# A two-layer mixer block: modulation sums on VectorE, neighbourhood q and k projected in transposed form, and recurrent gates whose sigmoid follows in SBUF

## The chip, the cores and the metric

The kernel runs on one core of one Trainium2 chip. The metric is the device time of one execution in microseconds (us), as the median of several runs; the profile is of one execution of its own.

## The reference

Two layers work on 1024 latent tokens and 256 context tokens (1280 rows in all) of 1024 channels. Each layer is one modulated block:

```python
shift, scale, gate = split(silu(cond) @ w_mod + b_mod, 3)    # for c and for c_ctx: two streams
p = (layer_norm(x) * (1 + scale) + shift) @ w_in             # 7072 columns
ya = neighbourhood_attention(q, k, v)                        # A: 4 heads of 64, scale 1/8
yb = mla(...);  yc = rglru(...);  yd = gqa(...)              # B, C, D
out = sum(sigmoid(m[i]) * ((y[i] * silu(z[i])) @ w_branch[i]) for i in range(4)) @ w_out
x = layer_norm(alpha * x + gate * out) * ln_g + ln_b
```

Branch C is a gated linear recurrence in both directions: `r = sigmoid(x @ w_a + b_a)`, `i = sigmoid(x @ w_x + b_x)`, `a = exp(-8 r softplus(-lambda))`, `u = sqrt(1 - a*a) * i * x`, and a scan `h = a h + u`. The second layer needs no context output, so its merge has 1024 rows where the first has 1280.

## The kernel before

Everything is float32. Most matrix products are made of three TensorE products of rounded parts (`mm_a`, L297 to L301, with the x tile standing and the weights moving; `mm_b`, L303 to L309, with the weights standing and x moving): a high part made by a ScalarE copy (`hi`) and a low part, the difference, made by VectorE (`lo`). Weights come from HBM in pieces of 128x512 (SP's queue, L278), are split in the same way (L263 on ScalarE, L264 on VectorE), and have two raw buffers and six pairs of split ones in the later half of a layer.

A layer runs through these stages, with the names that the trace shows: `g_proj`; then `m_proj`, `a_proj` (both projections of the branches) woven with `lru` (branch C); then the attentions `g_att`, `m_att`, `a_att`; then `merge` (gates, branch products and their sum), `last` and `outp`. `weave` runs two generators in turn by the given weights, which only sets the order of recording; a scheduler then reorders within what dependencies allow, and each engine works through its own list in order.

*Modulation.* The first modulation is made at the start. The other three (gate of layer 0, shift and scale of layer 1, gate of layer 1; 4096 columns in all) are made by `later_mods`, woven into the merge of layer 0. For each of 64 pieces of `w_mod` (tile `wm`, three buffers of the tag `q`), the two condition columns `sc` stand in TensorE and the weights move through (L188). At the end ScalarE copies the two rows out of PSUM (L194), 32 small transposes turn them into columns (L197), and VectorE adds the bias (L199). The second layer's merge has none of this.

*Neighbourhood projection.* `a_steps` projects q and k of branch A for each tile of 128 rows with x standing, copies them out of PSUM on ScalarE (L808, L809), turns each 128x128 block by a TensorE transpose (`put_t`, L348), splits it and writes both parts to HBM, since the attention wants channels on the partitions.

*Recurrent branch.* For each of two channel halves and two directions, two gates are made. Each has three products of 256, 512 and 512 columns in PSUM, and the sigmoid with its bias takes each out (L515). Then follow Tanh (L522), Exp (L523) and Sqrt (L528) on 128x1280. ScalarE loads a function table (ACT_TABLE_LOAD) where the next function isn't in the loaded one.

*Merge.* For each of four branches and eight output chunks `c`: with a gate chunk not made ahead, 24 products of x with gate weights per group of rows (`merge__mm`), then 6 of the branch (`wide`, three banks of PSUM used in turn). ScalarE makes the sigmoid (L999). VectorE multiplies (L1003 in the first branch, L1005 later), and VectorE or GpSimd adds to the sum `acc` (L1006: GpSimd for the chunks whose gate was made ahead).

Of the kernel before, what the change touches and what calls it, by code (L numbers as in the profile page):

```python
# [8 lines left out]
F32 = mybir.dt.float32  # L9
F32R = mybir.dt.float32r  # L10
AF = mybir.ActivationFunctionType
ALU = mybir.AluOpType
# [24 lines left out]
W_A = 30  # L37
# [10 lines left out]
def hybrid_kernel(ctx: ExitStack, tc, a):  # L48
# [124 lines left out]
    def modulation(l, base, ncols, out, stage, sw):  # L173
# [18 lines left out]
        for j in range(g):  # L192
            row = tmp()
            act.copy(row[0:2, :w_], acc[32 * j:32 * j + 2, :w_])  # L194
            for i in range(w_ // 128):
# [5 lines left out]
                          bm[:, :n, None].to_broadcast([128, n, 2]), ALU.add)  # L201
        if n == 16:
            dve.tensor_scalar(mc[:, :, 8:16], mc[:, :, 8:16], 1.0, None, ALU.add)
# [111 lines left out]
    def layer(l, xh, xl, need_ctx, gate, finish, side, ahead=None):  # L315
# [157 lines left out]
        def lru_steps():  # L473
            cw, cb, ba, bx, ca, cn = lru["cols"][l]
            for c in range(2):
# [30 lines left out]
                for d in range(2):  # L506
                    ri = []
                    for gi, bias in enumerate((ba, bx)):
                        wh, wl = gh[:, 2 * d + gi, :], gl[:, 2 * d + gi, :]
                        o = slot(s="lrug")  # L510
                        for g in groups:
                            gs = slice(g[0], g[0] + g[1])
                            ps = sbank()
                            mm_b(ps[:, :g[1]], [(wh, wl)], lambda k: (xch[:, gs], xcl[:, gs]))
                            act.activation(o[:, gs], ps[:, :g[1]], AF.Sigmoid, bias=bias[:, 2 * d + c:2 * d + c + 1])  # L515
                        ri.append(o)
                        yield
                    r, i = ri
# [282 lines left out]
        def a_steps():  # L801
            wa = load_rows(w_in, C_A, 512)
            prev = None
            for t, ps in project(wa, lambda t: 0 if t >= q0t else 256, 512):
                c0 = 0 if t >= q0t else 256
                y = tmp()
                if c0 == 0:
                    act.activation(y[:, :256], ps[:, :256], AF.Copy, scale=0.125)  # L808
                act.copy(y[:, 256:], ps[:, 256:])  # L809
                if prev:  # L810
                    put_t(*prev)
                prev = qk_a, t, c0 // 128, [y[:, c:c + 128] for c in range(c0, 512, 128)]
                yield
            put_t(*prev)
# [196 lines left out]
        weave((f"merge{l}", merge(), 4 * KC * len(qgroups)), (f"mod{l}", side, 68))  # L1011
# [150 lines left out]
    def raw_w():  # L1162
        return tp.tile([128, 512], F32, tag="q", name=nm("wm"), bufs=3)

    def later_mods():
        yield from modulation(0, 2048, 1024, gate0, raw_w, 512)
        yield from modulation(1, 0, 2048, mc1, raw_w, 512)
        yield from modulation(1, 2048, 1024, gate1, raw_w, 512)
# [102 lines left out]
```

## Time and profile before

| | |
|---|---|
| median of 3 runs | 2924.19 us (2923.29 to 2927.37) |
| profiled execution | 2926.0 us, of which the span is 2924.2 us |
| mean granted TensorE clock | 0.979 |
| TensorE busy | 2782.2 us (95%) |
| VectorE, ScalarE, GpSimd busy | 1503.1, 1219.3, 420.1 us |
| merge of layer 0 | 1082.3 to 1486.3 us of the span |
| merge of layer 1 | 2540.0 to 2823.4 us of the span |

The span runs from the first to the last instruction of the profiled execution. An engine's busy time is the sum over its instructions, and of a fraction of the span; what an engine off the path does costs nothing by itself, so a stage's own rows have to be read.

### The profile page before, as it was taken

Reading aid. Unit: us, or ns where it says so; the run is one execution under the profiler, and the core shown is the slowest. Engines: PE = TensorE matmul, PEld = TensorE weight load, DVE = VectorE, ACT = ScalarE, POOL = GpSimd, SP = SyncE. Lnnn points to the kernel's source line nnn. Section 1 sums busy time; section 2 is a strip of 40 time slices with the busy share of each in tenths; the row PEclk is TensorE's granted clock in tenths of the full one; section 3 lists DMA queues with packets and bytes.
Section 4 is the critical chain, followed back from the end, with each engine's and each line's share of the span. In section 5 each row is a group of like instructions: output and inputs, shape, how many; then the busy total and the mean of one; then the engine's idle time right before and its main releaser. Section 6 shows DMA issues by size and latency. Waiting matters only on the chain. (4 is left out here: it accounts for less than half of the span.)

```text
span 2924.2 us, 40179 instructions
## 1 busy us (share of the span) xinstructions
PE 2782.2 (95%) x14458; PEld 2248.4 (77%) x14458; DVE 1503.1 (51%) x3085; ACT 1219.3 (42%) x2617; POOL 420.1 (14%) x507
## 2 busy tenths in 40 slices
PE   7978999999999999999999797999999999999998
PEld 4766788888888887777767586788888888777776
DVE  5645435555455652233358655445555556533357
ACT  4353535445455552222224435535545455522230
POOL 1211011110111100111222121011111111001131
PEclk9988999999999999999999898999999999999999
DMA  7424232222223324333332333342222333222232
GB/s 249 119 66 146 79 103 84 85 85 85 92 86 124 103 94 128 100 121 120 122 89 87 99 102 102 105 122 87 85 88 78 113 115 110 93 87 88 89 113 88
DMA packets 240424, 301.83 MB, mean 103 GB/s; under 512 B 27488, under 2 KB 160096, under 8 KB 240224
## 3 DMA queue, kind: packets, MB, share of 16 engines
q1 hardware_dynamic: 134368, 225.58, 24.5%
q10 hardware_dynamic: 105856, 73.68, 8.1%
q8 instruction: 114, 1.87, 0.3%
q14 instruction: 86, 0.70, 0.1%
HBM read 217.11 MB, written 82.07 MB: 102 GB/s over the span
## 5 line engine op out<-in xcount | busy, mean ns | idle before, releaser
L307 PE MATMUL merge__mm<-xh,merge__whi 128*128 128x512 f32 (+1 forms) x640 | 242.2, 378 | 0.9 <-ACT a_att__tmp L934 0.9
L308 PE MATMUL merge__mm<-xl,merge__whi 128*128 128x512 f32 (+1 forms) x640 | 238.6, 373 | 0.0
L309 PE MATMUL merge__mm<-xh,merge__wlo 128*128 128x512 f32 (+1 forms) x640 | 238.5, 373 | 0.0
L313 DVE TENSOR_TENSOR m_att__pl<-m_att__t,m_att__ph 128x384 fp32r<-128x384 f32 (+1 forms) x248 | 122.0, 508 | 117.5 <-ACT m_att__ph L312 78.8
L1005 DVE TENSOR_TENSOR merge__tmp<-wide,merge__tmp 128x512 f32<-128x512 f32 (+1 forms) x120 | 76.5, 637 | 194.8 <-PE wide L309 173.7
L263 ACT CAST merge__whi<-merge__wraw 128x256 fp32r<-128x256 f32 (+1 forms) x128 | 65.8, 514 | 249.3 <-PE merge__mm L308 172.9
L1006 POOL TENSOR_TENSOR merge__acc<-merge__acc,merge__tmp 128x512 f32<-128x512 f32 (+1 forms) x60 | 79.0, 1317 | 574.8 <-DVE merge__tmp L1005 574.7
L313 DVE TENSOR_TENSOR g_att__pl<-g_att__t,g_att__ph 128x384 fp32r<-128x384 f32 (+1 forms) x228 | 112.8, 515 | 88.3 <-ACT g_att__ph L312 56.0
L312 ACT CAST m_att__ph<-m_att__t 128x384 fp32r<-128x384 f32 (+1 forms) x248 | 105.2, 440 | 115.0 <-PE m_att__t L584 105.3
L307 PEld LDWEIGHTS merge__mm<-xh,merge__whi 128*128 128x128 f32 x640 | 120.2, 188 | 42.8 <-issue 16.5
L264 DVE TENSOR_TENSOR merge__wlo<-merge__wraw,merge__whi 128x256 fp32r<-128x256 f32 (+1 forms) x128 | 72.0, 563 | 131.8 <-ACT merge__whi L263 124.8
L309 PEld LDWEIGHTS merge__mm<-xh,merge__wlo 128*128 128x128 f32 x640 | 120.3, 188 | 23.8 <-issue 0.4
L308 PEld LDWEIGHTS merge__mm<-xl,merge__whi 128*128 128x128 f32 x640 | 120.3, 188 | 22.4
L307 PE MATMUL wide<-merge__uh,merge__whi 128*128 128x256 f32 (+1 forms) x320 | 127.9, 400 | 9.3 <-DVE merge__tmp L1005 6.7
L312 ACT CAST g_att__ph<-g_att__t 128x384 fp32r<-128x384 f32 (+1 forms) x228 | 98.2, 446 | 83.3 <-PE g_att__t L584 78.7
L307 PE MATMUL a_att__mm<-xh,a_att__whi 128*128 128x512 f32 (+1 forms) x320 | 123.7, 387 | 0.0
L641 DVE TENSOR_SCALAR_CACHE_REDUCE g_att__p<-wide 128x1280 f32<-128x1280 f32 (+1 forms) x72 | 98.6, 1369 | 45.9 <-PE wide L639 35.7
L641 DVE TENSOR_SCALAR_CACHE_REDUCE m_att__p<-wide 128x1280 f32<-128x1280 f32 (+1 forms) x72 | 98.7, 1371 | 42.3 <-PE wide L639 41.8
L309 PE MATMUL a_att__mm<-xh,a_att__wlo 128*128 128x512 f32 (+1 forms) x320 | 120.0, 377 | 0.0
L308 PE MATMUL a_att__mm<-xl,a_att__whi 128*128 128x512 f32 (+1 forms) x320 | 120.0, 375 | 0.0
L308 PE MATMUL wide<-merge__ul,merge__whi 128*128 128x256 f32 (+1 forms) x320 | 119.7, 374 | 0.0
L299 PE MATMUL a_proj__mm<-a_proj__whi,xh 128*128 128x256 f32 (+1 forms) x320 | 110.3, 346 | 9.9 <-ACT a_proj__whi L263 9.8
(418 smaller groups left out, 7908.4 us busy)
## 6 DMA issues: line engine op xcount, KB each, us to landing
merge__wraw<-in_w_chunks_dram SPq DMA_DIRECT2D x64, 256.0 KB, 2.9
mod__wm<-in_w_mod_dram SPq DMA_DIRECT2D x64, 256.0 KB, 3.1
g_proj__wm<-in_w_mod_dram SPq DMA_DIRECT2D x16, 512.0 KB, 9.6
a_att__wraw<-in_w_chunks_dram SPq DMA_DIRECT2D x32, 256.0 KB, 2.8
merge__wraw<-in_w_branch_dram SPq DMA_DIRECT2D x64, 128.0 KB, 2.0
merge__tmp<-start__gates SPq DMA_DIRECT2D x32, 256.0 KB, 3.2
merge__tmp<-outp__gates SPq DMA_DIRECT2D x32, 256.0 KB, 3.4
g_att__wraw<-in_w_chunks_dram SPq DMA_DIRECT2D x28, 256.0 KB, 2.7
```

Source lines behind the costliest of these rows:

```text
L263: act.copy(hi[:, :n], raw[:, :n])
L264: (pool if by_pool else dve).tensor_sub(lo[:, :n], raw[:, :n], hi[:, :n])
L299: pe.matmul(ps, xh, wh[:, n0:n1], start=first and k == 0, stop=False)
L307: pe.matmul(ps, wh, xh, start=first and k == 0, stop=False)
L308: pe.matmul(ps, wh, xl, start=False, stop=False)
L309: pe.matmul(ps, wl, xh, start=False, stop=last and k == nk - 1)
L312: act.copy(hi, src)
L313: dve.tensor_sub(lo, src, hi)
L641: dve.tensor_scalar(pt[:, :nk], wide[:, :nk], -scale, None, ALU.mult, ALU.min, accum_out=nb)
L1005: dve.tensor_mul(sgm[:, :g[1]], pb[:, :g[1]], sgm[:, :g[1]])
L1006: (pool if w is None else dve).tensor_add(acc[c][:, gs], acc[c][:, gs], sgm[:, :g[1]])
```

## The change

- `later_mods` calls a new `modulation_apart`. The condition values become per-partition factors on VectorE: per block of 512 columns and per stream, one TENSOR_SCALAR and seven SCALAR_TENSOR_TENSOR of 128x512 add the eight pieces of `w_mod` up (L223 and L225 of the changed kernel; sums in the tags `ph` and `pl`, three and two buffers). Four TensorE products per block and stream with the sum standing and one column of `mhalf` (each -0.5) moving add over the partitions (L230). One VectorE instruction applies -2 and the bias (L233). The steps' weight in the weave goes from 68 to 76, and W_A from 30 to 32.
- `a_steps` makes q and k with the weights standing (`mm_b`), so that channels come out on the partitions; ScalarE takes the high part out of PSUM, VectorE the low part, and two DMAs write them. The transposes and the copies ahead of them are gone for this branch.
- `lru` takes the gates out of PSUM with Identity and the bias (L548), and two sigmoids of 128x1280 in SBUF follow (L553).

```diff
-W_A = 30
+W_A = 32
...
+    def modulation_apart(l, base, ncols, out):
+        acc = ps_v.tile([128, 512], F32, tag="pv", name=nm("pm"))
+        n = ncols // 128
+        bm = lc.tile([128, 16], F32, tag="bm", name=nm("bm"))
+        sp.dma_start(bm[:, :n], a["b_mod"][l, :, base // 128:base // 128 + n])
+        for h in range(ncols // 512):
+            sums = [tp.tile([128, 512], F32, tag=tag, name=nm("ms"), bufs=b) for tag, b in (("ph", 3), ("pl", 2))]
+            for k in range(KC):
+                w = raw_w()
+                sp.dma_start(w, a["w_mod"][l, k * 128:(k + 1) * 128, base + h * 512:base + (h + 1) * 512])
+                for s in range(2):
+                    if k == 0:
+                        dve.tensor_scalar(sums[s], w, sc[:, k, s:s + 1], None, ALU.mult)
+                    else:
+                        dve.scalar_tensor_tensor(sums[s], w, sc[:, k, s:s + 1], sums[s], ALU.mult, ALU.add)
+                yield
+            for s in range(2):
+                for c in range(4):
+                    o = s * n + 4 * h + c
+                    pe.matmul(acc[:, o:o + 1], sums[s][:, c * 128:(c + 1) * 128], mhalf[:, 0:1], start=True, stop=True)
+            yield
+        mc = lc.tile([128, 2, 16], F32, tag="modc", name=nm("modc"), bufs=4)
+        dve.scalar_tensor_tensor(mc[:, :, :n], acc[:, :2 * n].rearrange("p (s n) -> p s n", s=2), -2.0,
+                                 bm[:, None, :n].to_broadcast([128, 2, n]), ALU.mult, ALU.add)
...
-                            act.activation(o[:, gs], ps[:, :g[1]], AF.Sigmoid, bias=bias[:, 2 * d + c:2 * d + c + 1])
+                            act.activation(o[:, gs], ps[:, :g[1]], AF.Identity, bias=bias[:, 2 * d + c:2 * d + c + 1])
                         ri.append(o)
                         yield
+                    for o in ri:
+                        act.activation(o, o, AF.Sigmoid)
...
         def a_steps():
             wa = load_rows(w_in, C_A, 512)
-            prev = None
-            for t, ps in project(wa, lambda t: 0 if t >= q0t else 256, 512):
-                c0 = 0 if t >= q0t else 256
-                y = tmp()
-                if c0 == 0:
-                    act.activation(y[:, :256], ps[:, :256], AF.Copy, scale=0.125)
-                act.copy(y[:, 256:], ps[:, 256:])
-                if prev:
-                    put_t(*prev)
-                prev = qk_a, t, c0 // 128, [y[:, c:c + 128] for c in range(c0, 512, 128)]
+            items = [(c, g) for c in range(4) for g in (qgroups if c < 2 else groups)]
+            def part(c, g, ps, ks):
+                xs = xs_g(g)
+                ws = [(wh[:, c * 128:(c + 1) * 128], wl[:, c * 128:(c + 1) * 128]) for wh, wl in wa]
+                mm_b(ps[:, :g[1]], [ws[k] for k in ks], lambda j: xs(ks[j]), ks[0] == 0, ks[-1] == KC - 1)
+            def keep(c, g, ps):
+                n, scale = g[1], 0.125 if c < 2 else 1.0
+                hi = tp.tile([128, 512], F32R, tag="ph", name=nm("th"), bufs=3)
+                lo = tp.tile([128, 512], F32R, tag="pl", name=nm("tl"), bufs=2)
+                act.activation(hi[:, :n], ps[:, :n], AF.Copy, scale=scale)
+                dve.scalar_tensor_tensor(lo[:, :n], ps[:, :n], scale, hi[:, :n], ALU.mult, ALU.subtract)
+                for d, s in enumerate((hi, lo)):
+                    act.dma_start(qk_a[d, c, :, g[0]:g[0] + n], s.bitcast(F32)[:, :n])
+            for c, g in items[:-2]:
+                ps = mm()
+                part(c, g, ps, list(range(KC)))
+                keep(c, g, ps)
                 yield
-            put_t(*prev)
...
-        weave((f"merge{l}", merge(), 4 * KC * len(qgroups)), (f"mod{l}", side, 68))
+        weave((f"merge{l}", merge(), 4 * KC * len(qgroups)), (f"mod{l}", side, 76))
...
     def later_mods():
-        yield from modulation(0, 2048, 1024, gate0, raw_w, 512)
-        yield from modulation(1, 0, 2048, mc1, raw_w, 512)
-        yield from modulation(1, 2048, 1024, gate1, raw_w, 512)
+        yield from modulation_apart(0, 2048, 1024, gate0)
+        yield from modulation_apart(1, 0, 2048, mc1)
+        yield from modulation_apart(1, 2048, 1024, gate1)
```

The scheduler's order changes with it. Below, a row is a line of the program, an operation, the tile written and the tiles read, with the columns of the output, in the order in which the engine takes them.

TensorE, before, some 20 us into the merge of layer 0 (between the first and the third chunk; `wide` is a branch product, L188 a modulation piece):

```order
L309 MATMUL wide<-merge__uh_10946,merge__wlo_10975 128x512
L188 MATMUL mod__pm_11013<-mod__wm_11109,sc 2x256 x2
L188 MATMUL mod__pm_11013<-mod__wm_11123,sc 2x256 x2
L188 MATMUL mod__pm_11013<-mod__wm_11137,sc 2x256
L307 MATMUL wide<-merge__uh_10932,merge__whi_11094 128x256
```

Three pieces of modulation stand between two branch products; such stops recur through the whole merge.

TensorE in the changed kernel, some 53 rows into the same merge (L340 to L342 are L307 to L309 of before):

```order
L341 MATMUL merge__mm_11013<-xl,merge__whi_10958 128x512
L342 MATMUL merge__mm_11013<-xh,merge__wlo_10959 128x512
L230 MATMUL mod__pm_11003<-mhalf,mod__ms_11006 128x1 x4
L230 MATMUL mod__pm_11003<-mhalf,mod__ms_11007 128x1 x4
L340 MATMUL merge__mm_11051<-xh,merge__whi_10952 128x512
```

No row of L188 is left in this merge; the rows of L230 are 16 in all, two for each of the eight blocks, and stand in seven places.

VectorE, before, in the merge's first branch (L1003 takes a `wide` bank out of PSUM, L264 makes the low part of weights):

```order
L1003 TENSOR_TENSOR merge__acc_10978<-wide,merge__tmp_11058 128x512
L264 TENSOR_TENSOR merge__wlo_11318<-merge__wraw_11315,merge__whi_11317 128x512
L1003 TENSOR_TENSOR merge__acc_11098<-wide,merge__tmp_11099 128x256
L1003 TENSOR_TENSOR merge__acc_11098<-wide,merge__tmp_11113 128x512
L1003 TENSOR_TENSOR merge__acc_11098<-wide,merge__tmp_11127 128x512
```

Nothing but the low parts of weights stands between the multiplications that free the banks.

VectorE in the changed kernel at the same place (L1056 is L1003 of before, L297 is L264):

```order
L1056 TENSOR_TENSOR merge__acc_10968<-wide,merge__tmp_11050 128x512
L297 TENSOR_TENSOR merge__wlo_11320<-merge__wraw_11317,merge__whi_11319 128x512
L225 SCALAR_TENSOR_TENSOR mod__ms_11756<-mod__wm_11796,sc,mod__ms_11756 128x512
L1056 TENSOR_TENSOR merge__acc_11094<-wide,merge__tmp_11095 128x256
L225 SCALAR_TENSOR_TENSOR mod__ms_11755<-mod__wm_11835,sc,mod__ms_11755 128x512
L225 SCALAR_TENSOR_TENSOR mod__ms_11756<-mod__wm_11835,sc,mod__ms_11756 128x512
L1056 TENSOR_TENSOR merge__acc_11094<-wide,merge__tmp_11109 128x512
L225 SCALAR_TENSOR_TENSOR mod__ms_11755<-mod__wm_11856,sc,mod__ms_11755 128x512
L225 SCALAR_TENSOR_TENSOR mod__ms_11756<-mod__wm_11856,sc,mod__ms_11756 128x512
L225 SCALAR_TENSOR_TENSOR mod__ms_11755<-mod__wm_11882,sc,mod__ms_11755 128x512
L1056 TENSOR_TENSOR merge__acc_11094<-wide,merge__tmp_11119 128x512
```

Each PSUM bank that VectorE frees now has modulation sums ahead of it. They begin some 45 rows ahead of the first L1056, among the last instructions of `a_att`: from there to the second group of the merge's third chunk, 49 of the 128 sums stand in VectorE's list, and 25 of the 64 pieces of `w_mod` belong to them.

ScalarE, before, in one direction of the recurrent branch:

```order
L515 ACTIVATE lru__lrug_1628<-wide,lrucols 128x512
L523 ACT_TABLE_LOAD
L523 ACTIVATE lru__lrug_1524<-lru__lrug_1524,lrusp_311 128x1280
L515 ACT_TABLE_LOAD
L515 ACTIVATE lru__lrug_1628<-wide,lrucols 128x512
```

The last eviction of the second gate stands behind the Exp and a table load of its own.

ScalarE in the changed kernel at the same place (L548 is L515 of before, L559 is L523; L756 and L789 belong to `m_proj`):

```order
L548 ACTIVATE lru__lrug_1628<-wide,lrucols 128x512
L559 ACT_TABLE_LOAD
L559 ACTIVATE lru__lrug_1615<-lru__lrug_1615,lrusp_311 128x1280
L548 ACTIVATE lru__lrug_1628<-wide,lrucols 128x512
L756 ACTIVATE m_proj__tmp_1887,m_proj__ss_377_1888<-m_proj__mm_1862 128x128
L553 ACT_TABLE_LOAD
L553 ACTIVATE lru__lrug_1628<-lru__lrug_1628 128x1280
L789 COPY m_proj__mbuf_1690<-wide 128x256
```

The eviction after the Exp no longer has a table load ahead of it; the load stands ahead of the sigmoid, and both stand ahead of a copy of `m_proj`. Both programs have 39 table loads on ScalarE.

## Rows read from the trace of the kernel before

**Rows 1.** The page, busy time of TensorE, share of the span, instructions.

```profile
...
PE 2782.2 (95%) x14458; PEld 2248.4 (77%) x14458; DVE 1503.1 (51%) x3085; ACT 1219.3 (42%) x2617; POOL 420.1 (14%) x507
```

**Rows 2.** Busy time by stretch: stretch, length, engines, granted clock, DMA share, GB/s.

```profile
...
117.00:265.00 148.00, 125.67 (x611) 105.66 (x609) 78.26 (x178) 68.02 (x165) 28.05 (x45) 0.91 0.34 96
...
1082.30:1486.30 404.00, 398.49 (x1972) 297.40 (x1970) 144.81 (x249) 113.01 (x239) 57.99 (x53) 0.99 0.39 120
...
2540.00:2823.40 283.40, 278.07 (x1161) 216.22 (x1162) 117.68 (x188) 91.08 (x176) 44.94 (x35) 0.99 0.31 97
```

**Rows 3.** The same view of the first merge, tiles mod__pm, then mod__t alone.

```profile
...
1082.30:1486.30 404.00, 39.62 (x192) 5.41 (x192) 5.20 (x12) 0.99 0.39 120
...
1082.30:1486.30 404.00, 3.88 (x32) 2.94 (x32) 0.58 (x3) 0.99 0.39 120
```

**Rows 4.** Timeline of TensorE in the first merge: start, duration, engine, line, operation.

```profile
...
1118.87 0.39 PE L309 MATMUL wide<-merge__uh,merge__wlo 128*128 128x512 f32 x1
1119.19 0.60 PE L188 MATMUL mod__pm<-mod__wm,sc 128*2 128x256 f32 x4
1119.72 0.50 PE L307 MATMUL merge__mm<-xh,merge__whi 128*128 128x512 f32 x1
1120.06 0.40 PE L308 MATMUL merge__mm<-xl,merge__whi 128*128 128x512 f32 x1
```

**Rows 5.** Waits of TensorE in the first merge: us, times, longest.

```profile
...
PE wide L307 <- DVE merge__tmp L1005: 3.2, 5, 0.8
```

**Rows 6.** Instructions of L1077: count, duration min/median/max in ns.

```profile
...
L1077 DVE SCALAR_TENSOR_TENSOR outp__Y<-outp__Y,outp__mv,outp__ln_g x36: 735/748/756, 1528.0 to 2918.6; 128x512 f32<-128x512 f32 x36
```

**Rows 7.** Busy time by stretch, around the start of the first merge.

```profile
...
1062.00:1119.00 57.00, 56.23 (x302) 44.70 (x300) 18.90 (x36) 15.94 (x32) 1.23 (x2) 1.00 0.38 125
```

**Rows 8.** Loads of the tile mod__wm.

```profile
...
DMA to landing us min/median/max: 2.5/3.1/9.1
```

**Rows 9.** Instructions of L1006 in the first merge, durations in ns.

```profile
...
L1006 DVE TENSOR_TENSOR merge__acc<-merge__acc,merge__tmp x36: 424/685/1225, 1186.9 to 1476.0; 128x512 f32<-128x512 f32 x24, 128x256 f32<-128x256 f32 x12
L1006 POOL TENSOR_TENSOR merge__acc<-merge__acc,merge__tmp x34: 727/1296/1806, 1203.5 to 1478.0; 128x512 f32<-128x512 f32 x22, 128x256 f32<-128x256 f32 x12
```

**Rows 10.** Waits of SP's queue in the first merge.

```profile
...
SPq L278 <- DVE merge__wlo L264: 136.8, 39, 10.3
SPq L185 <- PE mod__pm L188: 106.6, 34, 8.1
```

**Rows 11.** Busy time of the tile a_proj__t in both layers.

```profile
...
sum 558.00, PE 13.06 PEld 9.45 DVE 13.13 ACT 11.57; mean PE 6.53 PEld 4.73 DVE 6.56 ACT 5.78
```

**Rows 12.** Timeline of TensorE around one set of those transposes.

```profile
...
294.28 0.60 PE L348 MATMUL a_proj__t<-ident,a_proj__tmp 128*128 128x128 f32 x4
294.63 0.48 PE L307 MATMUL wide<-xh,lru__whi 128*128 128x512 f32 x1
294.96 0.40 PE L308 MATMUL wide<-xl,lru__whi 128*128 128x512 f32 x1
```

**Rows 13.** Waits of TensorE, projections of the first layer.

```profile
...
PE a_proj__mm L299 <- ACT a_proj__whi L263: 9.8, 4, 6.2
PE wide L299 <- ACT lru__lrug L515: 6.7, 2, 3.7
...
PE wide L307 <- ACT lru__lrug L515: 1.7, 1, 1.7
```

**Rows 14.** Waits of TensorE, projections of the second layer.

```profile
...
PE wide L299 <- ACT lru__lrug L515: 3.0, 1, 3.0
PE wide L307 <- ACT lru__lrug L515: 2.6, 2, 1.7
```

**Rows 15.** Timeline of ScalarE, one direction of the recurrent branch.

```profile
...
185.30 1.28 ACT L515 ACT_TABLE_LOAD   x1
186.59 0.69 ACT L515 ACTIVATE lru__lrug<-wide,lrucols 128x512 f32<-128x512 f32 x1
...
189.29 1.27 ACT L528 ACTIVATE lru__lrut<-lru__lrut 128x1280 f32<-128x1280 f32 x1
```

More of the change, by code (lines that the diff above doesn't have):

```diff
@@ L201, in modulation, with raw_w @@
                           bm[:, :n, None].to_broadcast([128, n, 2]), ALU.add)
+        if n == 16:
+            dve.tensor_scalar(mc[:, :, 8:16], mc[:, :, 8:16], 1.0, None, ALU.add)
+        out["m"] = mc
+        yield
+    def raw_w():
+        return tp.tile([128, 512], F32, tag="q", name=nm("wm"), bufs=3)
+    def modulation_apart(l, base, ncols, out):
[18 more added lines that the diff above has]
+                    pe.matmul(acc[:, o:o + 1], sums[s][:, c * 128:(c + 1) * 128], mhalf[:, 0:1], start=True, stop=True)
+            yield
+        mc = lc.tile([128, 2, 16], F32, tag="modc", name=nm("modc"), bufs=4)
+        dve.scalar_tensor_tensor(mc[:, :, :n], acc[:, :2 * n].rearrange("p (s n) -> p s n", s=2), -2.0,
+                                 bm[:, None, :n].to_broadcast([128, 2, n]), ALU.mult, ALU.add)
         if n == 16:
@@ L802, in a_steps @@
             wa = load_rows(w_in, C_A, 512)
-            prev = None
-            for t, ps in project(wa, lambda t: 0 if t >= q0t else 256, 512):
-                c0 = 0 if t >= q0t else 256
-                y = tmp()
-                if c0 == 0:
-                    act.activation(y[:, :256], ps[:, :256], AF.Copy, scale=0.125)
-                act.copy(y[:, 256:], ps[:, 256:])
-                if prev:
-                    put_t(*prev)
-                prev = qk_a, t, c0 // 128, [y[:, c:c + 128] for c in range(c0, 512, 128)]
-                yield
-            put_t(*prev)
+            items = [(c, g) for c in range(4) for g in (qgroups if c < 2 else groups)]
[15 more added lines that the diff above has]
+                keep(c, g, ps)
+                yield
+            last = [(c, g, mm()) for c, g in items[-2:]]
+            for k in range(KC):
+                for c, g, ps in last:
+                    part(c, g, ps, [k])
+            for c, g, ps in last:
+                keep(c, g, ps)
+                yield
             wv = load_rows(w_in, C_AV, 256)
@@ L1160, in hybrid_kernel @@
     x1 = dr.tile([SEQ, D], F32, name="x1", bufs=1)
-    def raw_w():
-        return tp.tile([128, 512], F32, tag="q", name=nm("wm"), bufs=3)
     def later_mods():
-        yield from modulation(0, 2048, 1024, gate0, raw_w, 512)
-        yield from modulation(1, 0, 2048, mc1, raw_w, 512)
-        yield from modulation(1, 2048, 1024, gate1, raw_w, 512)
+        yield from modulation_apart(0, 2048, 1024, gate0)
+        yield from modulation_apart(1, 0, 2048, mc1)
+        yield from modulation_apart(1, 2048, 1024, gate1)
     def fin0(t, Y, later):
```

## The prediction

> **What bounds the kernel now.** The page's first part: TensorE is busy for 95% of the span [rows 1], so a microsecond off its list is a microsecond off the end unless something else comes late. The stretches show where there is room [rows 2]: the merge of layer 0 keeps TensorE busy for 398.5 of 404.0 us at clock 0.99, with VectorE at 144.8 us there; the woven projections (117 to 265 us) hold idle time and a clock of 0.91. The merge of layer 1 is the same work on 1024 rows instead of 1280, without modulations: 283.4 x 1.25 = 354, so 50 us of the first merge belong to something else. I read the change against these stretches, from whose own time of 2926.0 us I work; the median of the runs is 1.8 us lower.
>
> **The modulations leave TensorE: -48.** Their 192 instructions (two for a product) are busy for 39.6 us and the 32 transposes for 3.9 [rows 3], 43.5 together. Each stop also costs its neighbour: behind the stop at 1119.19 the next product starts at 1119.72 and the one behind that 0.34 us later, not 0.23 as in this stream elsewhere [rows 4], so 0.1 each; I count 47 stops, 4.7 us. The sum, 48, agrees with the 50 us above. None of it was hidden, since TensorE stands still in this merge for a few us only [rows 5].
>
> **What comes back on TensorE: +12.** 64 products of one column, in two passes like those before: 128 passes, each with another 128x128 block standing. Before has no such shape. The nearest is the transpose of 128x128, also with a block of its own each: four of them are followed by the next product 0.35 us after their start (294.28 to 294.63), 0.09 each, or 0.15 by their busy time of 0.60 [rows 12]. So 11 to 19 us; below, with a single pass each, 5.6. I take 0.09, since the passes follow one another without a wait for one another, and add 0.1 at each of seven places: 12.
>
> **VectorE gets the sums: +10 at the start of the merge.** 112 instructions of SCALAR_TENSOR_TENSOR on 128x512 with both inputs in SBUF and a factor per partition: 0.748 us, the same form at L1077 [rows 6]. The 16 TENSOR_SCALAR read one input less; at the same price as an upper bound, 128 x 0.748 = 96 us. VectorE then has 145 + 96 = 241 us in a merge of some 365: no bound on average. But the order decides. From the last instructions of `a_att` to the second group of the merge's third chunk, 49 sums stand in VectorE's list. In before this stretch is 1062 to 1119 us: VectorE has 18.9 us there and TensorE 56.2 of 57.0 [rows 7]. With 49 x 0.748 = 36.7 VectorE has 55.6 us of work in a stretch that gets some us shorter without its stops. It is full, and each of its 25 pieces of `w_mod` comes over three buffers, with 3.1 us from issue to landing [rows 8], 9.1 at worst; a pair of sums takes 1.5 us, so three buffers give a piece every (3.1 + 1.5)/3 = 1.5 us at best. Queued behind the sums are the multiplications that free the three `wide` banks and the low parts of weights, and TensorE waits for both. VectorE's excess alone is a few us; a handful of late landings of 3 to 6 us more makes it 20. I take 10, between 0 (TensorE runs up to three banks ahead) and 25. Behind this place the sums thin out, and the 16 rows on TensorE stand far behind their sums.
>
> **SP's queue.** The same 64 pieces of 256 KB are loaded. SP waits for a free `wm` 106.6 us in this merge already, and 136.8 us for weights' buffers, without TensorE noticing [rows 5, 10]: nothing, covered by the six pairs of split weights. If that cover is gone, it is the third rival.
>
> **The neighbourhood transposes: -11.** The products keep their columns (for both layers the same sum over chunks and groups, three products each). What goes is 76 transposes, busy for 13.1 us in both layers [rows 11]. In the timeline four of them hold the stream for 0.35 us and the next product for 0.1 [rows 12]; from start to start over all 26 sets I get 11.0. Bounds 9 and 13. ScalarE loses 38 copies, which TensorE waits for hardly at all. With weights standing, the first group has 256 columns and needs all eight pieces of the weights in half the time that a tile of 512 columns took; TensorE waits for those weights 9.8 us in layer 0 [rows 13]. That can grow by half a group, up to 3 us; I take 1.5. So -9.5.
>
> **The gates: 0.** Sixteen sigmoids of 128x1280 are new. The nearest is the Sqrt of the same size, 1.27 us [rows 15]: 20 us more ScalarE. The table loads do not change in number, 39 as before; what changes is which instruction waits behind one. The eviction behind the Exp had 1.28 us of load ahead of it [rows 15], now not: 8 x 1.28 = 10 us earlier. TensorE waits for these evictions 6.7 + 1.7 us in layer 0 and 3.0 + 2.6 in layer 1 [rows 13, 14], 14.0 in all, so at best -14. Against it, `m_proj`'s copies stand behind a sigmoid that was not there: 8 x 1.27 = 10 us late, at worst 20 with both sigmoids in each. Equal prices, opposite signs: 0, from -14 to +20.
>
> **Sum.** -48 + 12 + 10 - 9.5 + 0 = -35.5. 2926.0 - 35.5 = 2890.5, less 1.8: **2889 us**. Its own range, with the bounds of the terms taken as independent, is 2875 to 2903. Chance 0.52.
>
> **Rivals.**
> 1. *VectorE is late again in the later branches.* From the second branch on GpSimd adds too, and the two already slow each other: VectorE's add at L1006 takes 0.685 us in the middle and 1.225 at worst, GpSimd's 1.296 and 1.806 [rows 9]. For it: the sums have both inputs in SBUF like that add. Against it: 241 us in 365. If each of 34 GpSimd adds costs a sum the difference of 0.54 us, and TensorE sees all, 18 us come back: 2907. Chance 0.17. The Trainium skill, page "SBUF — State Buffer", section "Who interferes with whom", says that a VectorE instruction with two SBUF inputs and a GpSimd instruction that reads SBUF exclude each other for a whole instruction. The stretched durations of both agree with it; by it all of GpSimd's 58 us could be lost to VectorE, which then has 299 us of work in the same stretch.
> 2. *The gates and the clock give time.* If the 14 us of waits for gate evictions vanish, and the projections keep a better clock than 0.91 with fewer stops, 14 to 25 us more: about 2870. For it: ScalarE's list loses a load at the right place. Against it: `m_proj` waits for ScalarE as well. Chance 0.15.
> 3. *The loads of `w_mod` hold up the merge's weights (the other side).* SP takes its list in order; a piece now comes free only when VectorE, which has other work, has done both its sums. If TensorE stands still for t at each of 64 pieces, the gain is gone at 64t = 35.5 + 10, t = 0.7 us; at a pair of sums, 1.5 us, 96 us are lost against 45.5 gained: 2926.0 - 45.5 + 96 - 1.8 = 2975. For it: one queue, three buffers. Against it: the 243 us that SP waits now cost nothing. Chance 0.06 for slower than before, 0.04 for a loss that about eats the gain.
> 4. *The sigmoids delay `m_proj`*: +10 to +20, 2899 to 2909. Chance 0.06. That part of the change would then do the opposite of freeing PSUM early; that the loads stay at 39 speaks for it.
>
> **Chances.** 0.52 + 0.17 + 0.15 + 0.06 = 0.90 faster by over 0.2% (5.8 us, about what a measurement of this kernel can tell from no change); 0.04 within it; 0.06 slower. The range reaches from beyond the second rival to beyond the first and the fourth, and leaves out the third and what is left of its cases: **2860 to 2911**.
>
> **What would show it.** In the first merge: no row of L188, the stretch near 370 us, rows of L230 of about 0.09 us each, and VectorE at some 240 us. TensorE's waits in its first 40 us name VectorE (the bank's multiplication, a low part, or L230 for a sum) and come to about 10 us. In `a_proj` no transposes, the two stretches about 10 us shorter together. In `lru` the waits for gate evictions fall, those for `m_proj`'s copies rise. I am wrong if TensorE waits all through the merge (rival 1 or 3, told apart by whether SP or VectorE is the one that is late), or if L230 costs over 0.2 us a pass.

## The result, and the profile after

The changed kernel takes 2904.14 us (median of 4 runs, 2902.22 to 2908.94) and the kernel before, on the same chip, 2925.01 us. The ratio is 0.9931, with a 95% interval of 0.9913 to 0.9948: faster by 0.7%, 21 us. The forecast was 2889, 35.5 us less, with a range of 2860 to 2911.

First the page of the changed kernel, busy time and share of the span by engine; it answers to [rows 1].

```profile
span 2900.4 us, 40048 instructions
...
PE 2740.0 (94%) x14334; PEld 2251.1 (78%) x14334; DVE 1587.9 (55%) x3215; ACT 1221.5 (42%) x2585; POOL 416.3 (14%) x507
```

TensorE lost 42 us of work, the span 24. Busy time by stretch tells where the rest went: the projections of layer 0 in two pieces, the merge of layer 0, the projections of layer 1 in two pieces, the merge of layer 1, and behind them the sum of the four pieces of projections from a second cut. A row has the stretch, its length, the busy time (instructions) of TensorE, its weight loads, VectorE, ScalarE and GpSimd, then the granted clock, the DMA share and GB/s.

```profile
117.50:269.00 151.50, 126.89 (x629) 108.48 (x627) 80.41 (x182) 74.61 (x174) 25.05 (x45) 0.89 0.35 99
269.00:410.50 141.50, 124.75 (x691) 106.87 (x690) 49.31 (x66) 52.29 (x76) 0.52 (x1) 0.94 0.30 97
...
1082.50:1461.00 378.50, 364.61 (x1869) 301.66 (x1868) 219.75 (x361) 108.51 (x225) 58.78 (x51) 1.00 0.42 125
...
1670.30:1798.70 128.40, 108.16 (x530) 92.56 (x528) 69.00 (x156) 63.61 (x147) 24.99 (x43) 0.88 0.32 92
1798.70:1933.00 134.30, 122.52 (x675) 103.19 (x674) 54.94 (x81) 57.31 (x90) 0.53 (x1) 0.97 0.36 115
...
2516.80:2799.70 282.90, 278.16 (x1161) 216.35 (x1162) 118.03 (x188) 90.83 (x177) 44.84 (x35) 0.99 0.30 97
...
sum 555.70, PE 482.32 PEld 411.10 DVE 253.66 ACT 247.81 POOL 51.09; mean PE 120.58 PEld 102.77 DVE 63.42 ACT 61.95 POOL 12.77
```

The reader is to see two things. The first merge is 25.5 us shorter than in [rows 2] (378.5 after 404.0), which is the whole gain of this execution. And the projections, cut in the same way, are as long as before: 555.7 us, where before had this sum.

```profile
sum 555.50, PE 492.83 PEld 415.42 DVE 253.50 ACT 239.74 POOL 56.59; mean PE 123.21 PEld 103.86 DVE 63.38 ACT 59.93 POOL 14.15
```

TensorE has 10.5 us less to do there, and stands still 10.7 us longer: 73.4 us after 62.7 (length less busy time). ScalarE has 8 us more, although this branch's copies are gone.

In the merge, the one-column products (stretch view of the tile `mod__pm`, the waits of TensorE, and the view of instructions for L230 and L225; durations in ns are min/median/max):

```profile
1082.50:1461.00 378.50, 14.67 (x128) 15.37 (x128) 0.52 (x3) 1.00 0.42 125
```

```profile
PE wide L340 <- DVE merge__tmp L1058: 10.7, 11, 2.5
PE wide L340 <- ACT merge__uh L345: 1.9, 2, 1.4
PE wide L340 <- DVE merge__acc L1056: 0.9, 1, 0.9
```

```profile
L230 PE MATMUL mod__pm<-mhalf,mod__ms x128: 164/250/251, 1094.2 to 1453.6; 128*128 128x1 f32 x128
```

```profile
L225 DVE SCALAR_TENSOR_TENSOR mod__ms<-mod__wm,sc,mod__ms x112: 731/746/1792, 1068.1 to 1367.4; 128x512 f32<-128x512 f32 x112
```

128 passes are busy for 14.7 us, 0.115 each. TensorE's waits are 13.5 us, of which 11.6 for VectorE's multiplications, where [rows 5] had 3.2; only 0.9 of them are for L1056, the multiplication of the first branch where I had expected them.

### The profile page after: what moved, and what is told of

It reads as the page before. It is cut to its first block, busy times and chain, and to the rows that moved or that the text cites. A ratio compares the mean times of both kernels' runs of the same rounds, so it can differ in the third digit from the quotient of the medians.

```text
span 2900.4 us, 40048 instructions
## 1 busy us (share of the span) xinstructions
PE 2740.0 (94%) x14334; PEld 2251.1 (78%) x14334; DVE 1587.9 (55%) x3215; ACT 1221.5 (42%) x2585; POOL 416.3 (14%) x507
## 5 line engine op out<-in xcount | busy, mean ns | idle before, releaser
L340 PE MATMUL merge__mm<-xh,merge__whi 128*128 128x512 f32 (+1 forms) x640 | 239.5, 374 | 0.9 <-ACT a_att__tmp L987 0.9
L342 PE MATMUL merge__mm<-xh,merge__wlo 128*128 128x512 f32 (+1 forms) x640 | 238.8, 373 | 0.0
L340 PE MATMUL wide<-merge__uh,merge__whi 128*128 128x256 f32 (+1 forms) x320 | 128.8, 402 | 18.6 <-DVE merge__tmp L1058 14.2
L340 PEld LDWEIGHTS merge__mm<-xh,merge__whi 128*128 128x128 f32 x640 | 120.4, 188 | 24.3 <-ACT a_att__tmp L987 1.4
L342 PEld LDWEIGHTS merge__mm<-xh,merge__wlo 128*128 128x128 f32 x640 | 120.6, 188 | 23.1
L297 DVE TENSOR_TENSOR merge__wlo<-merge__wraw,merge__whi 128x256 fp32r<-128x256 f32 (+1 forms) x128 | 71.8, 562 | 100.2 <-ACT merge__whi L296 95.5
L340 PE MATMUL a_att__mm<-xh,a_att__whi 128*128 128x512 f32 (+1 forms) x320 | 123.8, 387 | 0.0
L342 PE MATMUL a_att__mm<-xh,a_att__wlo 128*128 128x512 f32 (+1 forms) x320 | 120.0, 376 | 0.0
L342 PE MATMUL wide<-merge__uh,merge__wlo 128*128 128x256 f32 (+1 forms) x320 | 118.7, 371 | 0.0
```

Source lines behind the costliest of these rows:

```text
L297: (pool if by_pool else dve).tensor_sub(lo[:, :n], raw[:, :n], hi[:, :n])
L340: pe.matmul(ps, wh, xh, start=first and k == 0, stop=False)
L342: pe.matmul(ps, wl, xh, start=False, stop=last and k == nk - 1)
```

## The experiments

Four kernels take the change apart. They ran in turn with the kernel before (2927.2 us there).

**The modulations alone** (the `lru` and `a_steps` of before, W_A 30):

```diff
-        weave((f"merge{l}", merge(), 4 * KC * len(qgroups)), (f"mod{l}", side, 68))
+        weave((f"merge{l}", merge(), 4 * KC * len(qgroups)), (f"mod{l}", side, 76))
...
-        yield from modulation(0, 2048, 1024, gate0, raw_w, 512)
+        yield from modulation_apart(0, 2048, 1024, gate0)
```

> The kernel before with the modulation part of the change alone. The changed kernel's merge of layer 0 is 25.5 us shorter in the trace (378.5 after 404.0), and its projections together are not. Theory 1 (the projections' two parts cancel: the transposes give about 10, the sigmoids in SBUF take about 10) and theory 2 (neither of them does anything) both expect 24 to 27 us less than before here, about 2899. If the projections lose by something that the modulations do (order of the whole program), it would be less than 20.

2903.7 us, ratio 0.9918 (0.9904 to 0.9931): 23.5 us less. As both expected, a little short of it. Its merge, cut in the same way:

```profile
1082.00:1465.80 383.80, 368.36 (x1868) 305.40 (x1867) 220.71 (x361) 108.15 (x225) 58.87 (x51) 0.98 0.43 124
```

The same merge is 5.3 us longer here than in the changed kernel, at a granted clock of 0.98 for 1.00; TensorE is busy for 368.4 us in place of 364.6. So one trace tells the merge's gain only to some 5 us: 20.2 here, 25.5 there.

**The neighbourhood projection alone** (the new `a_steps`, W_A 32):

```diff
-W_A = 30
+W_A = 32
...
-            for t, ps in project(wa, lambda t: 0 if t >= q0t else 256, 512):
+            items = [(c, g) for c in range(4) for g in (qgroups if c < 2 else groups)]
```

> The kernel before with the neighbourhood projection in transposed form alone (and W_A 32). Theory 1: about 10 us less than before, 2915. Theory 2: the gain of 11 us is eaten by the first matrix products waiting for their weights (7.2 us once in each layer in the changed kernel, where layer 1 had none), so 2921 to 2927, no change.

2911.4 us, 0.9950 (0.9937 to 0.9962): 15.8 us less. Theory 2 falls here; theory 1 named too little.

**The gates alone:**

```diff
-act.activation(o[:, gs], ps[:, :g[1]], AF.Sigmoid, bias=bias[:, 2 * d + c:2 * d + c + 1])
+act.activation(o[:, gs], ps[:, :g[1]], AF.Identity, bias=bias[:, 2 * d + c:2 * d + c + 1])
...
+                    for o in ri:
+                        act.activation(o, o, AF.Sigmoid)
```

> The kernel before with Identity at the eviction and two sigmoids in SBUF alone. Theory 1: about 10 us more than before, 2935: the waits for gate evictions fall by 7 of 14 us, but transposes in m_proj wait for a low part that stands behind the sigmoids (two waits of 3 to 4 us in each layer of the changed kernel, 15 us). Theory 2: no change, 2922 to 2928.

2944.6 us, 1.0056 (1.0042 to 1.0069): 17.4 us more. The sum of the pieces of projections in its trace, cut as above:

```profile
sum 571.80, PE 497.14 PEld 420.43 DVE 253.24 ACT 258.37 POOL 53.32; mean PE 124.28 PEld 105.11 DVE 63.31 ACT 64.59 POOL 13.33
```

The loss lies there: 571.8 us for 555.5, with 18.6 us more ScalarE.

**The changed kernel without the gates part** (Sigmoid at the eviction, the two lines of the edit above taken out):

> The changed kernel with the sigmoid at the eviction as before, so the modulations and the neighbourhood projection alone. Theory 1: 2890 to 2894, 10 to 14 us less than the changed kernel. Theory 2: as the changed kernel, 2900 to 2906.

2890.5 us, 0.9872 (0.9859 to 0.9886). Theory 1 holds: 13.6 us less than the changed kernel's own median, and 36.7 less than before. (Against the kernel before of its own turn the changed kernel has -20.9, so between the two there are 13.6 to 15.8 us.) The three parts alone give -23.5 - 15.8 + 17.4 = -21.9; the changed kernel has -20.9. The pieces of projections, for comparison with what follows:

```profile
sum 542.50, PE 483.06 PEld 409.88 DVE 252.23 ACT 230.09 POOL 52.21; mean PE 120.77 PEld 102.47 DVE 63.06 ACT 57.52 POOL 13.05
```

Next, why the gates cost. Four more, all edits of the kernel without the gates part, in another turn with the kernel before (2926.55 us there).

**The first gate's sigmoid alone in SBUF:**

```diff
+act.activation(o[:, gs], ps[:, :g[1]], AF.Identity if gi == 0 else AF.Sigmoid, bias=bias[:, 2 * d + c:2 * d + c + 1])
...
+                        if gi == 0:
+                            act.activation(o, o, AF.Sigmoid)
```

> The changed kernel with only the first gate's sigmoid moved to SBUF (Identity at its eviction), the second as before. Against the changed kernel without the gates part (2890.5) and with it (2904.1 and, alone, 17 us). Theory S (the loss is ScalarE's added work, 1.27 us for each sigmoid in SBUF, that stands ahead of the projections' copies): half of the loss, 2897 to 2901. Theory L (the loss is the longer way of a gate, the table load that now stands between eviction and sigmoid): with one gate's sigmoid still at the eviction the load has its old place, so no more than 3 us, 2889 to 2894.

2893.6 us, 0.9893 (0.9879 to 0.9908): 3 us more than without the part. That lies in the range of theory L and below that of theory S: half of the added ScalarE work does not cost half of the loss. The sum of its pieces of projections:

```profile
sum 542.70, PE 481.83 PEld 409.04 DVE 251.72 ACT 239.82 POOL 53.42; mean PE 120.46 PEld 102.26 DVE 62.93 ACT 59.96 POOL 13.36
```

ScalarE has 9.7 us more than without the part, and the length is the same (542.7 and 542.5).

**VectorE takes the gates out of PSUM:**

```diff
-act.activation(o[:, gs], ps[:, :g[1]], AF.Sigmoid, bias=bias[:, 2 * d + c:2 * d + c + 1])
+dve.tensor_scalar(o[:, gs], ps[:, :g[1]], bias[:, 2 * d + c:2 * d + c + 1], None, ALU.add)
...
+                    for o in ri:
+                        act.activation(o, o, AF.Sigmoid)
```

> The changed kernel with VectorE taking the gates out of PSUM and adding the bias; both sigmoids in SBUF on ScalarE. ScalarE then has 16 x 1.27 = 20 us of sigmoids for the 16 x 1.85 = 30 us of evictions that the kernel without the gates part has, VectorE 30 us more. Theory S: nothing is lost, 2883 to 2893. Theory L: the way of a gate is as long as in the changed kernel, so 2900 to 2908.

2888.8 us, 0.9874 (0.9858 to 0.9889). Nothing is lost, with the same steps on a gate's way (out of PSUM, table load, sigmoid in SBUF) as in the changed kernel. Theory L falls too, so neither holds as it was put. The sum of its pieces of projections, and its longest waits of TensorE in layer 0:

```profile
sum 538.30, PE 478.60 PEld 408.81 DVE 281.15 ACT 223.99 POOL 49.66; mean PE 119.65 PEld 102.20 DVE 70.29 ACT 56.00 POOL 12.41
```

```profile
PE a_proj__mm L340 <- ACT a_proj__whi L296: 7.7, 1, 7.7
PE m_proj__t L381 <- DVE m_proj__tl L346: 7.1, 2, 4.3
```

The second row is a correction of theory 1: I had named these transposes in `m_proj` as the place of the loss, and they wait nearly as long here (12.5 us in both layers, 15.3 in the changed kernel), where nothing is lost.

**An Identity in place on each gate, behind sigmoids at the eviction:**

```diff
+                    for o in ri:
+                        act.activation(o, o, AF.Identity)
```

> The changed kernel with the sigmoids at the eviction, as before, and an Identity of 128x1280 in place on each gate behind them: the added ScalarE work without a moved function or table load (the Identity leaves the values as they are). Theory S: the whole loss comes back, 2902 to 2910. Theory L: 2889 to 2895.

2906.6 us, 0.9935 (0.9921 to 0.9948): 16 us more than without it. ScalarE work added at this place costs by itself what the moved sigmoids cost, whatever its function and with no table load moved.

```profile
sum 557.10, PE 488.04 PEld 415.20 DVE 253.82 ACT 249.31 POOL 49.48; mean PE 122.01 PEld 103.80 DVE 63.46 ACT 62.33 POOL 12.37
```

**All adds of the first merge on VectorE:**

```diff
-(pool if w is None else dve).tensor_add(acc[c][:, gs], acc[c][:, gs], sgm[:, :g[1]])
+(pool if w is None and l else dve).tensor_add(acc[c][:, gs], acc[c][:, gs], sgm[:, :g[1]])
```

> The changed kernel without the gates part (2890.5), and in the merge of layer 0 all adds to the sum on VectorE, none on GpSimd. In the changed kernel's merge TensorE waits 10.7 us for VectorE's multiplications, most where GpSimd adds too, and sums take up to 1.79 us there instead of 0.75. If the two hinder each other (first rival of the prediction): the waits go, 2880 to 2887, although VectorE gets 34 adds more, 20 us. If VectorE's list is simply too long there: 2892 to 2905.

2886.0 us, 0.9866 (0.9852 to 0.9879); the kernel without the gates part had 0.9872 (0.9859 to 0.9886), so the time alone does not settle it. The durations of the sums do, for one point:

```profile
L225 DVE SCALAR_TENSOR_TENSOR mod__ms<-mod__wm,sc,mod__ms x112: 739/746/753, 1055.3 to 1355.8; 128x512 f32<-128x512 f32 x112
```

The longest sum falls from 1.79 us (1.825 in the kernel without the gates part) to 0.753, so the two engines do hinder each other. TensorE's waits stay, though (7.7 us for L1056 of this kernel, the later branches' multiplication, and 2.6 for L1054, the first branch's; 9.9 and 1.3 without the edit), so this was not what made them.

The last four (2926.77 us for the kernel before there), again edits of the kernel without the gates part, ask for those waits and for the second gate.

**One stream's sums on VectorE:**

```diff
-            sums = [tp.tile([128, 512], F32, tag=tag, name=nm("ms"), bufs=b) for tag, b in (("ph", 3), ("pl", 2))]
+            sums = [tp.tile([128, 512], F32, tag=tag, name=nm("ms"), bufs=b) for tag, b in (("ph", 3),)]
...
-                for s in range(2):
+                for s in range(1):
...
-                    pe.matmul(acc[:, o:o + 1], sums[s][:, c * 128:(c + 1) * 128], mhalf[:, 0:1], start=True, stop=True)
+                    pe.matmul(acc[:, o:o + 1], sums[0][:, c * 128:(c + 1) * 128], mhalf[:, 0:1], start=True, stop=True)
```

> The changed kernel without the gates part (2890.5), with the sums of the first stream alone on VectorE; both streams' one-column products read the first stream's sums, so the modulation of the context rows is that of the latent rows. All 64 loads and 128 passes stay, VectorE has 64 sums fewer, 48 us. If TensorE's waits of about 13 us in this merge come from VectorE's work: they fall below 5, 2879 to 2884. If they come from the loads in SP's queue: 2888 to 2892.

2908.9 us, 0.9945 (0.9933 to 0.9958): 18 us slower with half of the sums, which neither expected. One wait is 11 of them. Timelines of TensorE and VectorE, then of the DMA queues from 1094 to 1108 us the packets and the issues (tile, count, KB each, median us from issue to landing):

```profile
1114.15 0.58 PE L340 MATMUL wide<-merge__uh,merge__whi 128*128 128x256 f32 x1 [11.24 <-DVE merge__acc L1054]
```

```profile
1105.86 0.75 DVE L225 SCALAR_TENSOR_TENSOR mod__ms<-mod__wm,sc,mod__ms 128x512 f32<-128x512 f32 x1 [7.40 <-DMA mod__wm<-in_w_mod_dram]
1112.02 0.48 DVE L223 TENSOR_SCALAR mod__ms<-mod__wm,sc 128x512 f32<-128x512 f32 x1 [5.41 <-DMA mod__wm<-in_w_mod_dram]
...
1113.41 0.68 DVE L1054 TENSOR_TENSOR merge__acc<-wide,merge__tmp 128x512 f32<-128x512 f32 x1
```

```profile
DMA packets 1743, 0.88 MB, mean 63 GB/s; under 512 B 1325, under 2 KB 1325, under 8 KB 1742
...
mod__wm<-in_w_mod_dram SPq DMA_DIRECT2D x3, 256.0 KB, 14.6
merge__wraw<-in_w_chunks_dram SPq DMA_DIRECT2D x1, 256.0 KB, 14.5
...
last__gate<-mod__modc SPq DMA_DIRECT2D x1, 4.0 KB, 18.0
```

VectorE stands 7.4 and 5.4 us for pieces to land, with the multiplication that frees TensorE's bank behind them. A landing takes 14.6 us here, where its median over this kernel is 3.2. What lies ahead of these loads in the queue is the write of a finished gate to HBM (`last__gate`), 4 KB in small packets: 1325 of the 1743 packets of this stretch are under 512 B, and all queues together move 63 GB/s. With half of the sums the first gate is done earlier, at the start of the merge, and its write meets the loads there. TensorE's granted clock is 0.77 from 1100 to 1130 us too. So this run doesn't tell what VectorE's work costs by itself; it shows a third party.

**One load for each block:**

```diff
-                w = raw_w()
-                sp.dma_start(w, a["w_mod"][l, k * 128:(k + 1) * 128, base + h * 512:base + (h + 1) * 512])
+                if k == 0:
+                    w = raw_w()
+                    sp.dma_start(w, a["w_mod"][l, k * 128:(k + 1) * 128, base + h * 512:base + (h + 1) * 512])
```

> The changed kernel without the gates part (2890.5), with one load of w_mod for each block of 512 columns, whose tile all eight steps read: 8 loads in place of 64, so the modulations are not those of the reference; the 128 sums and 128 passes stay. The longest wait in the changed kernel's merge (2.54 us at 1201.66) follows from four such loads that hold SP for 10.6 us ahead of a weight of the merge. If the loads in SP's queue are the cause: waits below 5, 2879 to 2884. If VectorE's work is: 2888 to 2892, or more, since the sums then come in a denser row.

2884.4 us, 0.9856 (0.9842 to 0.9869), at the edge of the forecast for the loads; the interval overlaps that of the kernel without the gates part (0.9859 to 0.9886). The merge of the profiled execution is 373.5 us long, 383.7 in the kernel without the gates part; of these 10.2 us TensorE's idle time is 5.7 (8.0 after 13.7), and the rest is its busy time, at a granted clock of 0.99 after 0.98. TensorE waits 7.6 us, of which for VectorE's multiplication:

```profile
PE wide L341 <- DVE merge__tmp L1057: 5.6, 9, 0.9
```

No wait for it is over 0.9 us (2.8 without the edit), so the long ones hang on the loads; the short ones stay with VectorE.

**The second gate's sigmoid alone in SBUF** (as the first gate's, with `gi == 1`):

> The changed kernel with only the second gate's sigmoid moved to SBUF. The first gate's cost 3 us by itself (2893.6), both cost 13.6 (2904.1). If each of the sigmoids costs by its place: the second, which stands behind the last eviction with a table load of its own ahead of the Sqrt, costs the rest, 2899 to 2904. If the two cost only together (a sum that passes a cover): about 3 us too, 2892 to 2896.

2897.6 us, 0.9893 (0.9878 to 0.9908): 7 us by the medians, 3 for the first gate, 13.6 for both. The runs of this kernel spread from 2890.3 to 2898.5, so a share of its own and a share of the two together are not told apart.

**A version from the findings**, the whole change with the gates taken out by VectorE and the first merge's adds on VectorE:

> A version from the findings: all parts of the change, with VectorE taking the gates out of PSUM (2888.8) and all adds of the first merge on VectorE (2886.0 for that alone, against 2890.5). If the two gains of 2 and 4.5 us add up: 2882 to 2886. If either was only between two runs of a kernel: 2886 to 2891.

2885.0 us, 0.9856 (0.9842 to 0.9870): 42 us less than before and 19 less than the changed kernel. Against the same kernel without the moved adds (0.9874, 0.9858 to 0.9889) the difference is not settled.

## Why the prediction was right, and where it was off

**Modulations off TensorE, -48 + 12 + 10 = -26: right in sum.** The merge is 25.5 us shorter in the profiled execution, 20.2 in that of the part alone, and the part alone gives 23.5 by the medians. Of the terms, the one-column products were 14.7 us for the 12 taken, 0.115 a pass, between the two readings of the transposes' row (0.09 and 0.15). The lateness was 8.4 us for the 10 taken, as TensorE's idle time (13.9 us, from 5.5); that the size fits is luck, since the waits are not those that it was worked out from.

**Its place was wrong.** I had put it at the merge's start, from VectorE's 55.6 us of work in 57. VectorE did keep up there: 0.9 us. It came in the later branches, 5.1 us from 1180 to 1230 us and 5.6 behind that, so my sign of being wrong (waits all through the merge) was there, at a small price. The longest wait can be followed back through the timelines of the changed kernel, here from its end: TensorE, VectorE, ScalarE, SP's queue, and VectorE again.

```profile
1201.66 0.50 PE L340 MATMUL wide<-merge__uh,merge__whi 128*128 128x512 f32 x1 [2.54 <-DVE merge__tmp L1058]
```

```profile
1199.98 0.69 DVE L297 TENSOR_TENSOR merge__wlo<-merge__wraw,merge__whi 128x512 fp32r<-128x512 f32 x1 [2.71 <-ACT merge__whi L296]
1200.59 0.68 DVE L1059 TENSOR_TENSOR merge__acc<-merge__acc,merge__tmp 128x512 f32<-128x512 f32 x1
1201.19 0.42 DVE L1058 TENSOR_TENSOR merge__tmp<-wide,merge__tmp 128x256 f32<-128x256 f32 x1
```

```profile
1199.33 0.62 ACT L296 CAST merge__whi<-merge__wraw 128x512 fp32r<-128x512 f32 x1 [6.49 <-DMA merge__wraw<-in_w_chunks_dram]
```

```profile
1176.24 1.06 SPq L1070 DMA_DIRECT2D last__gate<-mod__modc  x2
...
1182.10 10.64 SPq L220 DMA_DIRECT2D mod__wm<-in_w_mod_dram  x4
1196.35 0.33 SPq L311 DMA_DIRECT2D merge__wraw<-in_w_chunks_dram  x1
```

The waits of SP's queue from 1193 to 1197 us have one row, and it names VectorE:

```profile
SPq L311 <- DVE merge__wlo L297: 3.9, 1, 3.9
```

```profile
1189.33 1.42 DVE L225 SCALAR_TENSOR_TENSOR mod__ms<-mod__wm,sc,mod__ms 128x512 f32<-128x512 f32 x2 [5.00 <-DMA mod__wm<-in_w_mod_dram]
...
1195.24 0.75 DVE L225 SCALAR_TENSOR_TENSOR mod__ms<-mod__wm,sc,mod__ms 128x512 f32<-128x512 f32 x1 [0.34 <-DMA mod__wm<-in_w_mod_dram]
1195.91 0.75 DVE L297 TENSOR_TENSOR merge__wlo<-merge__wraw,merge__whi 128x256 fp32r<-128x256 f32 x2
```

The multiplication that frees the bank stands behind the low part of a weight, that behind ScalarE, and ScalarE waits 6.5 us for the weight. SP issued it late, at 1196.35. Four loads of `w_mod` ahead of it had taken 10.6 us, but they were through at 1192.7; what held the weight after that was its raw buffer, 3.9 us, which an earlier low part on VectorE had to free. That low part stood behind modulation sums in VectorE's list, and VectorE had stood 5.0 us for their piece to land. So the forecast of the run with one load for each block, which put this wait down to SP being held by the four loads, had one link wrong. At 1176.24 two gate writes had gone into the queue. In the DMA view from 1174 to 1198 us a piece takes 6.6 us to land by the median, for 2.9 over the kernel:

```profile
mod__wm<-in_w_mod_dram SPq DMA_DIRECT2D x7, 256.0 KB, 6.6
...
last__gate<-mod__modc SPq DMA_DIRECT2D x2, 4.0 KB, 9.9
```

So "TensorE waits for VectorE" is, followed back, a late landing that both lists, VectorE's and SP's, pass on. It is near the third rival's way, at a few us in place of 96: the term "SP's queue: nothing" was wrong, not VectorE's load at the start. This is one wait followed back; the others over 0.9 us are tied to the loads only by their going in the kernel with one load for each block. That the gate writes make the landings slow is read from traces in which both stand together. In six kernels (before, changed, modulations alone, without the gates part, adds on VectorE, one load for each block), cut into windows of 15 us from 1100 to 1295 us, the pieces land after 5.9 to 8.1 us by the median in the window that holds the gate writes, and after 2.6 to 4.7 in the others. No run without the writes was made, and before has the same writes (6.0 us there), where TensorE did not notice them.

**The first rival** (VectorE and GpSimd hinder each other) is shown in the sums' durations, 1.79 us at worst and 0.753 without GpSimd's adds. The rule of the Trainium skill, page "SBUF — State Buffer", section "Who interferes with whom", agrees with these rows. Its price, 18 us, is not there: the kernel with the adds moved gains 4.5 us by the medians, inside the intervals.

**Transposes, -9.5: the size was off, -15.8.** The terms that were mis-sized are the transposes (-11) and the first weights (+1.5). The stretches of that kernel show a length 15.4 us less than before, and 9.8 us less ScalarE:

```profile
sum 540.10, PE 479.99 PEld 407.44 DVE 252.06 ACT 229.90 POOL 52.06; mean PE 120.00 PEld 101.86 DVE 63.02 ACT 57.48 POOL 13.01
```

TensorE's own work is 12.8 us less, and its idle time 2.6 us less, where the two terms had 11 less and 1.5 more. Whether the copies that ScalarE lost have a share in it, no run tells. In layer 0 the wait for the first weights, for which I had added 1.5 us, fell from 9.8 us [rows 13] to 1.0.

```profile
PE a_proj__mm L299 <- ACT a_proj__whi L263: 1.0, 1, 1.0
```

It is not gone for good: layer 1 of this kernel has one of 8.1 us for the first weights of `lru`, and the changed kernel waits 7.1 and 7.2 us for those of `a_proj`, one in each layer, where before had none in layer 1.

**Gates, 0: wrong, +17.4 alone and +13.6 beside the others.** This is the step on which the forecast of 35.5 lost its 15 us. It set two delays of 10 us against each other; the result lies near the far end of the bounds that it gave, -14 to +20. The gain was there, in part: the waits for gate evictions, 14.0 us in [rows 13, 14], are 7.1 in the changed kernel (4.1 + 2.3 + 0.7). The other side was not 10 us of one copy behind one sigmoid, but more than the gain. ScalarE's list is what the two woven streams of this stage share, and with both gates most of what is added to it comes out at the end; with one of them it does not. The sums say it, length of the projections beside ScalarE's busy time:

| kernel | ScalarE busy, us | length, us |
|---|---|---|
| gates out by VectorE | 224.0 | 538.3 |
| neighbourhood projection alone | 229.9 | 540.1 |
| changed, without the gates part | 230.1 | 542.5 |
| second gate's sigmoid in SBUF | 238.7 | 546.9 |
| before | 239.7 | 555.5 |
| first gate's sigmoid in SBUF | 239.8 | 542.7 |
| changed | 247.8 | 555.7 |
| Identity added | 249.3 | 557.1 |
| gates alone | 258.4 | 571.8 |

The two kernels with transposes (before and gates alone) have 492.8 and 497.1 us of TensorE's own work there, the others 478.6 to 488.0, so they are compared with each other only: 18.6 us more ScalarE make 16.3. Among the others the kernel without the gates part is the one to compare with (the neighbourhood projection alone has the same projections; that these two differ by 2.4 us shows how far a trace can be trusted). Both sigmoids, 17.7 us of ScalarE, make 13.2, and the Identity, 19.2 us, makes 14.6. The first gate's alone, 9.7 us, makes 0.2, and the second gate's alone, 8.6 us, makes 4.4. So the busy time of ScalarE by itself does not give the length: one gate's share is still covered, wholly or in part, and both together are not. The Identity that changes no value and no table is the direct test that it is the work and not the function: 16 us by the medians. That ScalarE is busy for less than half of this stage (248 of 556 us) had made me take it for free. What covers the first gate's share, and where along the two streams each microsecond is passed on to TensorE, stays open; the waits that the trace names do not tell it, as the row of `m_proj__t` showed.

The whole then is -23.5 - 15.8 + 17.4, where I had -26, -9.5 and 0. The fourth rival had the right size for the gates, at 0.06; that it is `m_proj` which they delay is not shown. The forecast came within its wide range because that held this rival's price, and because the transposes gave 6 us more than I had counted; the narrower range of the sum itself, 2875 to 2903, was just missed. So the whole came out near by luck in part: two terms of three were off, with opposite signs.

## What to carry to other kernels

Work added to an engine that is busy for less than half of a stage can still lengthen the stage, here where two woven streams share its list: add an instruction without effect to it and time that, before counting moved work as hidden. Test it at the full amount, since half of it was nearly free here. A sum over rows can leave TensorE at a good price (43.5 us of matrix products and transposes became 14.7 us there and, by the medians, 112 x 0.746 + 16 x 0.478 = 91 us on an engine with room); what then costs are its loads, in a queue that the stage's own weights share. A wait put down to one engine has to be followed back until something is not waiting.

## What the runs showed of the hardware

- Products of one column, each pass with another 128x128 block standing, took 0.115 us a pass, no less than before's transposes of 128 columns, also with a block of their own each (0.09 to 0.15 [rows 12]); a weight load beside it took 0.19 us.
- TENSOR_SCALAR on 128x512 in SBUF took 0.478 us, where SCALAR_TENSOR_TENSOR with a second tensor took 0.746:

```profile
L223 DVE TENSOR_SCALAR mod__ms<-mod__wm,sc x16: 471/478/710, 1067.0 to 1349.7; 128x512 f32<-128x512 f32 x16
```

- Identity asked for no function table here: the 48 evictions at L548 stand without one table load, where 15 stood at L515 of before. The loads went to the sigmoids in SBUF, so their number stayed:

```profile
L553 ACT ACTIVATE lru__lrug<-lru__lrug x16: 1269/1274/1277, 181.6 to 1887.0; 128x1280 f32<-128x1280 f32 x16
L553 ACT ACT_TABLE_LOAD  x15: 1283/1283/1283, 180.3 to 1885.7; - x15
```
